# Contrast adjustment on one core: last store in three pieces, first store begun with a piece of its own, bias matmuls in reverse order

## The chip, the cores and the metric

The kernel runs on one core of one Trainium2 chip. The metric is the device time of one execution in microseconds, as the median over several runs. The profile is of one further execution.

## The reference

The input is a batch of 16 images with 3 channels of 512 x 512 float32 pixels, 50.33 MB in all. For each image and channel the mean over its 262,144 pixels is taken, and each pixel is moved away from that mean by a factor of 1.5 and clipped to 0..1.

```python
def reference(x, factor):                       # x: (16, 3, 512, 512) float32, factor 1.5
    mean = np.mean(x, axis=(2, 3), keepdims=True)
    return np.clip(mean + factor * (x - mean), 0, 1).astype(np.float32)
```

## The kernel before

**Tiles.** The pixels are seen as one long row and cut into rows of `ROW` = 16384 floats (64 KB). One row fills one partition, 16 rows make one image channel, and 128 rows make a tile, so a tile is 8.39 MB and holds 8 channels. There are six tiles. Three buffers of a whole tile each (`BUFS` = 3) lie in SBUF, so tile t + 3 uses the buffer of tile t.

**Transfers.** `load` (L75 to L79) is issued by SyncE, named SP in the profile. The first tile is loaded by one DMA; each later one by two, the even rows and the odd rows (`PARTS` = 2), 64 rows of 64 KB each. `store` (L113 to L116) is issued by ScalarE's queue (ACT), also as even rows and odd rows. Loads and stores are thus in two queues, which share the 16 DMA engines; the profile calls them q1 (SP) and q10 (ACT). A tile's buffer is loaded anew as soon as the store of the same rows, three tiles before, has landed; SP waits for that, in its program's order.

**Compute of a tile.** `compute` (L81 to L111) first sums each row: VectorE (DVE) reduces the first 8192 columns (`HALF`) with one instruction into `sums` column 0 (L85), and ScalarE copies the other 8192 in four pieces of 2048 (`JUNK`) into a scratch tile `junk`, each with an accumulated sum into columns 1 to 4 (L91). Then TensorE (PE) multiplies `blockw` with each of the five columns of `sums` and accumulates into `pbias` (L96). `blockw` is a matrix with (1 - factor) / 262144 in blocks of 16 x 16 on its diagonal, so this sums the 16 rows of a channel and gives every row of it the bias (1 - factor) * mean. Each of the five matmuls is two instructions on PE. ScalarE copies the bias out of PSUM (L98).

The last step is factor * x + bias, clipped, in place. VectorE alone does columns 0 to 3839 (`OWN`): multiply and add (L100), then clip (L103). The other columns are in four pieces of 4096, 4096, 2816 and 1536 (`CHUNKS`): ScalarE makes Relu(factor * x + bias) of each (L109), and VectorE takes the minimum with 1 (L110), which is called the clamp below. The store of the tile follows the fourth piece.

**Order.** The instructions of each engine run in the order in which the program records them (`manual_schedule`): three loads, and then for each tile its compute, its store, and the load of the tile after next but one. The waits between engines, for data and for buffers, are put in by the framework. Each DMA counts its completion on one of eight counters, and the next DMA on the same counter waits until the one before it has landed.

Of the kernel before, what the change touches and what calls it, by code (L numbers as in the profile page):

```python
# [1 line left out]

# [4 lines left out]


P = 128  # L10
ROW = 16384
BUFS = 3
HALF = ROW // 2
OWN = 3840
CHUNKS = (4096, 4096, 2816, 1536)
JUNK = 2048
PARTS = 2


@with_exitstack  # L20
def kernel(
    ctx: ExitStack,
    tc: tile.TileContext,
    x: bass.AP,
    factor: float,
    out: bass.AP,
):

    nc = tc.nc
    f32 = mybir.dt.float32
    Alu = mybir.AluOpType
    Act = mybir.ActivationFunctionType

    B, C, H, W = x.shape
    n_img, n_pix = B * C, H * W
    ppi = n_pix // ROW
    per_tile = P // ppi
    n_tiles = n_img // per_tile  # L40
    assert OWN + sum(CHUNKS) == ROW
    assert ppi * ROW == n_pix and per_tile * n_tiles == n_img

    factor = float(factor)
    wconst = (1.0 - factor) / float(n_pix)

    x_f = x.rearrange("b c h w -> (b c h w)")
    out_f = out.rearrange("b c h w -> (b c h w)")

    def dram(ap, t, r, parts):  # L50
        return bass.AP(
            tensor=ap.tensor, offset=(t * P + r) * ROW, ap=[[parts * ROW, P // parts], [1, ROW]]
        )

    consts = ctx.enter_context(tc.tile_pool(name="consts", bufs=1))
    xpool = ctx.enter_context(tc.tile_pool(name="xpool", bufs=1))
    jpool = ctx.enter_context(tc.tile_pool(name="jpool", bufs=1))
    rpool = ctx.enter_context(tc.tile_pool(name="rpool", bufs=2))
    bpool = ctx.enter_context(tc.tile_pool(name="bpool", bufs=2))
    psum = ctx.enter_context(tc.tile_pool(name="psum", bufs=2, space=bass.MemoryType.PSUM))  # L60

    blockw = consts.tile([P, P], f32, name="blockw")
    nc.gpsimd.memset(blockw, 0.0)  # L65
    for a in range(0, P, 2 * ppi):
        mid, end = a + ppi, a + 2 * ppi
        nc.gpsimd.memset(blockw[a:end, mid:end], wconst)  # L68
        nc.gpsimd.memset(blockw[a:mid, mid:end], 0.0)  # L69
        nc.gpsimd.memset(blockw[a:mid, a:mid], wconst)  # L70


    bufs = [xpool.tile([P, ROW], f32, name=f"x{b}") for b in range(BUFS)]

    def load(t):  # L75
        xt = bufs[t % BUFS]
        parts = 1 if t == 0 else PARTS
        for r in range(parts):
            nc.sync.dma_start(out=xt[r::parts, :], in_=dram(x_f, t, r, parts))  # L79

    def compute(t):  # L81
        xt = bufs[t % BUFS]
        n_act = (ROW - HALF) // JUNK
        sums = rpool.tile([P, 1 + n_act], f32, name="sums")
        nc.vector.tensor_reduce(  # L85
            out=sums[:, 0:1], in_=xt[:, 0:HALF], axis=mybir.AxisListType.X, op=Alu.add
        )
        for j in range(n_act):
            junk = jpool.tile([P, JUNK], f32, name="junk")
            a = HALF + j * JUNK  # L90
            nc.scalar.activation(  # L91
                out=junk, in_=xt[:, a : a + JUNK], func=Act.Copy, accum_out=sums[:, 1 + j : 2 + j]
            )
        pbias = psum.tile([P, 1], f32, name="pbias")
        for j in range(1 + n_act):
            nc.tensor.matmul(pbias, blockw, sums[:, j : j + 1], start=j == 0, stop=j == n_act)  # L96
        bias = bpool.tile([P, 1], f32, name="bias")
        nc.scalar.copy(out=bias, in_=pbias)  # L98
        own = xt[:, 0:OWN]
        nc.vector.tensor_scalar(  # L100
            out=own, in0=own, scalar1=factor, scalar2=bias, op0=Alu.mult, op1=Alu.add
        )
        nc.vector.tensor_scalar(  # L103
            out=own, in0=own, scalar1=0.0, scalar2=1.0, op0=Alu.max, op1=Alu.min
        )
        c = OWN
        for n in CHUNKS:
            part = xt[:, c : c + n]
            nc.scalar.activation(out=part, in_=part, func=Act.Relu, bias=bias, scale=factor)  # L109
            nc.vector.tensor_scalar(out=part, in0=part, scalar1=1.0, scalar2=None, op0=Alu.min)  # L110
            c += n  # L111

    def store(t):  # L113
        xt = bufs[t % BUFS]
        for r in range(PARTS):
            nc.scalar.dma_start(out=dram(out_f, t, r, PARTS), in_=xt[r::PARTS, :])  # L116

    with tc.manual_schedule():
        for t in range(min(BUFS, n_tiles)):
            load(t)  # L120
        for t in range(n_tiles):
            compute(t)
            store(t)
            if t + BUFS < n_tiles:
                load(t + BUFS)


# [1 line left out]
_INS = ['x', 'factor']  # L129
_OUTS = [((16, 3, 512, 512), 'float32')]  # L130

_NUMBERS = {'factor': 1.5}


# [26 lines left out]
```

## Time and profile before

| | |
|---|---|
| time, median of 5 runs | 241.49 us (241.22, 241.47, 241.49, 243.47, 247.09) |
| the profiled execution's own time | 240.45 us |
| its span, first to last instruction | 238.4 us |
| granted TensorE clock | 1.00 |
| busy, VectorE / ScalarE / TensorE | 120.3 / 118.1 / 13.7 us |
| moved by the load queue / the store queue | 50.33 / 50.33 MB |
| mean rate over the span | 422 GB/s |
| one reduction of 8192 columns on VectorE (L85) | 8.68 us |
| one sum of 2048 columns on ScalarE (L91), and reading it out | 1.91 us, 0.19 us |
| the five matmuls of a tile (L96) | 2.3 us |
| one Relu of 4096 columns on ScalarE (L109) | 3.70 us |
| one clamp of 4096 columns on VectorE (L110) | 2.29 us |
| one issue of a store on ScalarE's queue (median) | 0.57 us |

The span is shorter than the execution's time by 2.05 us, which lie before the first and after the last instruction. Times in the profile are microseconds from the start of the span. The name of an engine with a q behind it (ACTq, SPq) stands for what its instruction queue does, such as issuing DMAs and waiting for semaphores, and isn't counted as busy time. Landing is the moment at which a DMA's last completion has been counted.

### The profile page before, as it was taken

The numbers are of one execution on the slowest core, as the hardware profiler recorded it, in microseconds if no ns is written. First come the engines' busy times: TensorE is split into PE (matmuls) and PEld (weight loads), VectorE is DVE, ScalarE is ACT, GpSimd is POOL, SyncE is SP. The second block draws the span as 40 slices with busy tenths as digits, with TensorE's granted clock in tenths as the row PEclk, the third lists the DMA queues.
The fourth block names the chain that finished last, engine by engine and source line by source line (L and its number), as shares of the span: only waits on it lengthen the run. The fifth ranks groups of instructions, "written<-read, shape, count | busy, mean of one in ns | idle before, by whom it ended". The sixth has DMA issues, their size and how long they took to land.

```text
span 238.4 us, 354 instructions
## 1 busy us (share of the span) xinstructions
PE 13.7 (6%) x60; PEld 13.3 (6%) x60; DVE 120.3 (50%) x42; ACT 118.1 (50%) x79; POOL 1.4 (1%) x17
## 2 busy tenths in 40 slices
PE   0000030003000030000012000003000001100000
PEld 0000030003000030000012000003000001100000
DVE  0001958995874958400687830195870068783000
ACT  2001949697954959300677910194960066791000
POOL 2000000000000000000000000000000000000000
DMA  9898989899999898989898989999898989898894
GB/s 352 352 528 352 528 352 528 352 352 484 396 451 429 385 495 352 528 352 528 352 518 363 495 385 484 396 429 451 385 495 352 528 352 517 363 517 363 352 528 176
DMA packets 1905, 100.67 MB, mean 422 GB/s; under 512 B 368, under 2 KB 368, under 8 KB 368
## 3 DMA queue, kind: packets, MB, share of 16 engines
q1 hardware_dynamic: 944, 50.33, 49.6%
q10 hardware_dynamic: 960, 50.33, 48.8%
q14 instruction: 1, 0.01, 0.0%
HBM read 50.33 MB, written 50.33 MB: 422 GB/s over the span
## 4 chain that ended last, share of the span: by engine, by line
DMA 34%; DVE 18%; ACT 17%; another core or an unknown queue 10%; issue 7%; PE 4%; DVEq 0%; SPq 0%
DMA out_dram<-x 20%; ACT x L109 16%; DVE sums L85 15%; DMA x<-in_x_dram 14%; PE pbias L96 4%; DVE x L110 4%; DVEq L156 0%; ACT bias L98 0%; SPq L79 0%; DVEq L85 0%
## 5 line engine op out<-in xcount | busy, mean ns | idle before, releaser
L85 DVE TENSOR_REDUCE sums<-x 128x1 f32<-128x8192 f32 x6 | 52.1, 8684 | 74.6 <-DMA x<-in_x_dram 59.7
L91 ACT ACTIVATE junk<-x 128x2048 f32<-128x2048 f32 x24 | 45.8, 1910 | 79.6 <-DMA x<-in_x_dram 76.7
L109 ACT ACTIVATE x<-x,bias 128x4096 f32<-128x4096 f32 (+2 forms) x24 | 67.8, 2898 | 0.2
L110 DVE TENSOR_SCALAR x<-x 128x4096 f32<-128x4096 f32 (+2 forms) x24 | 42.5, 1790 | 5.8 <-ACT x L109 5.8
L96 PE MATMUL pbias<-sums,blockw 128*128 128x1 f32 x60 | 13.7, 354 | 190.1 <-DVE sums L85 190.1
L96 PEld LDWEIGHTS pbias<-sums,blockw 128*128 128x128 f32 x60 | 13.3, 329 | 190.5 <-DVE sums L85 158.9
L100 DVE TENSOR_SCALAR x<-x,bias 128x3840 f32<-128x3840 f32 x6 | 13.3, 2221 | 15.5 <-ACT bias L98 15.5
L103 DVE TENSOR_SCALAR x<-x 128x3840 f32<-128x3840 f32 x6 | 13.0, 2160 | 0.2
L98 ACT COPY bias<-pbias 128x1 f32<-128x1 f32 x6 | 1.0, 160 | 16.6 <-PE pbias L96 16.6
L91 ACT ACTIVATION_READ_ACCUMULATOR junk<-x 128x1 f32 x24 | 4.5, 186 | 0.0
L91 ACT ACT_TABLE_LOAD x1 | 1.3, 1283 | 0.7 <-PEq L142 0.7
L68 POOL MEMSET blockw<- 32x16 f32 x4 | 0.4, 104 | 0.2
L69 POOL MEMSET blockw<- 16x16 f32 x4 | 0.4, 104 | 0.2
L70 POOL MEMSET blockw<- 16x16 f32 x4 | 0.4, 104 | 0.0
L65 POOL MEMSET blockw<- 128x128 f32 x1 | 0.2, 206 | 0.3 <-POOLq L142 0.3
L142 POOL MEMSET const-bfloat16-1.0<- 128x1 bf16 x1 | 0.1, 112 | 0.0
L142 POOL MEMSET const-uint8-127<- 128x1 uint8 x1 | 0.1, 112 | 0.0
L142 POOL MEMSET const-float32-1.0<- 128x1 f32 x1 | 0.1, 108 | 0.0
L142 POOL MEMSET const-float32-0.0<- 128x1 f32 x1 | 0.1, 104 | 0.2 <-issue 0.2
## 6 DMA issues: line engine op xcount, KB each, us to landing
out_dram<-x ACTq DMA_DIRECT2D x12, 40.7
x<-in_x_dram SPq DMA_DIRECT2D x11, 26.1
```

The lines of the kernel that those rows point to most:

```text
L68: nc.gpsimd.memset(blockw[a:end, mid:end], wconst)
L69: nc.gpsimd.memset(blockw[a:mid, mid:end], 0.0)
L70: nc.gpsimd.memset(blockw[a:mid, a:mid], wconst)
L85: nc.vector.tensor_reduce(out=sums[:, 0:1], in_=xt[:, 0:HALF], axis=mybir.AxisListType.X, op=Alu.add)
L91: nc.scalar.activation(out=junk, in_=xt[:, a : a + JUNK], func=Act.Copy, accum_out=sums[:, 1 + j : 2 + j])
L96: nc.tensor.matmul(pbias, blockw, sums[:, j : j + 1], start=j == 0, stop=j == n_act)
L98: nc.scalar.copy(out=bias, in_=pbias)
L100: nc.vector.tensor_scalar(out=own, in0=own, scalar1=factor, scalar2=bias, op0=Alu.mult, op1=Alu.add)
L103: nc.vector.tensor_scalar(out=own, in0=own, scalar1=0.0, scalar2=1.0, op0=Alu.max, op1=Alu.min)
L109: nc.scalar.activation(out=part, in_=part, func=Act.Relu, bias=bias, scale=factor)
L110: nc.vector.tensor_scalar(out=part, in0=part, scalar1=1.0, scalar2=None, op0=Alu.min)
L142: nc = _bacc.Bacc("TRN2", target_bir_lowering=False, num_devices=1)
```

## The change

Three things are changed, and the arithmetic stays the same.

1. The five matmuls of each tile run in reverse order: first ScalarE's fourth sum, then its third, second and first, and VectorE's sum last.
2. The store of the last tile is three DMAs, over all 128 rows, cut by columns: 0 to 7935 (`EARLY` = 7936), behind the third Relu and clamp in the program; then, behind the fourth, 7936 to 12031 (`LATE` = 12032) and 12032 to 16383. Before it was even rows and odd rows, behind the fourth.
3. The store of the first tile begins with columns 0 to 3839 of the even rows (15 KB of each of 64 rows), as a DMA of its own behind the second Relu and clamp. The rest of the even rows and then the odd rows follow behind the fourth.

The stores of the other four tiles are as they were. `store` is now called from within `compute`, with a list of pieces.

```diff
+EARLY = OWN + CHUNKS[0]
+LATE = EARLY + CHUNKS[1]
...
-    def dram(ap, t, r, parts):
+    def dram(ap, t, r, parts, c0=0, c1=ROW):
         return bass.AP(
-            tensor=ap.tensor, offset=(t * P + r) * ROW, ap=[[parts * ROW, P // parts], [1, ROW]]
+            tensor=ap.tensor,
+            offset=(t * P + r) * ROW + c0,
+            ap=[[parts * ROW, P // parts], [1, c1 - c0]],
         )
...
+    def store(t, pieces):
+        xt = bufs[t % BUFS]
+        for r, parts, c0, c1 in pieces:
+            nc.scalar.dma_start(out=dram(out_f, t, r, parts, c0, c1), in_=xt[r::parts, c0:c1])
+    late = len(CHUNKS) - 1
+    def stores(t):
+        if t == n_tiles - 1:
+            return {
+                late - 1: [(0, 1, 0, EARLY)],
+                late: [(0, 1, EARLY, LATE), (0, 1, LATE, ROW)],
+            }
+        if t == 0:
+            rest = [(r, PARTS, 0, ROW) for r in range(1, PARTS)]
+            return {1: [(0, PARTS, 0, OWN)], late: [(0, PARTS, OWN, ROW)] + rest}
+        return {late: [(r, PARTS, 0, ROW) for r in range(PARTS)]}
...
-        for j in range(1 + n_act):
-            nc.tensor.matmul(pbias, blockw, sums[:, j : j + 1], start=j == 0, stop=j == n_act)
+        for j in range(n_act, -1, -1):
+            nc.tensor.matmul(pbias, blockw, sums[:, j : j + 1], start=j == n_act, stop=j == 0)
...
-        for n in CHUNKS:
+        for k, n in enumerate(CHUNKS):
...
             c += n
+            store(t, stores(t).get(k, []))
-    def store(t):
-        xt = bufs[t % BUFS]
-        for r in range(PARTS):
-            nc.scalar.dma_start(out=dram(out_f, t, r, PARTS), in_=xt[r::PARTS, :])
...
             compute(t)
-            store(t)
```

## The prediction

> **What bounds the kernel now.** I began with the page: busy shares, slices, queues.
>
> ```profile
> PE 13.7 (6%) x60; PEld 13.3 (6%) x60; DVE 120.3 (50%) x42; ACT 118.1 (50%) x79; POOL 1.4 (1%) x17
> ...
> DMA  9898989899999898989898989999898989898894
> ```
>
> The first line gives each engine's busy time: none is at work for more than half the span. In the second, a digit is the DMA engines' busy share, in tenths, in a fortieth of the span, 8 or 9 in all but the last. The kernel is bound by its transfers, so the question is where the 16 DMA engines stand still. Busy time by stretch says that.
>
> ```profile
> 46.00:52.00 6.00, 0.00 (x0) 0.00 (x0) 6.00 (x2) 4.17 (x5) 0.00 (x0) 1.00 0.90 295
> 52.00:216.00 164.00, 11.47 (x50) 11.05 (x50) 94.25 (x35) 93.22 (x61) 0.00 (x0) 1.00 1.00 434
> ```
>
> The last three columns are granted clock, DMA share and GB/s. A packet counts where it starts, so short stretches are rough, but from 52 to 216 us the share is 1.00. Nothing that an engine does there can shorten the time. What happens after 216 us I read from the stores' line: first the two stores of tile 4, then the two of tile 5, the last.
>
> ```profile
> L116 ACTq DMA_DIRECT2D out_dram<-x x2: 479/548/617, 177.8 to 178.3; - x2
> ...
> DMA to landing us min/median/max: 30.0/34.6/39.2
> ```
>
> ```profile
> L116 ACTq DMA_DIRECT2D out_dram<-x x2: 479/544/609, 216.4 to 216.9; - x2
> ...
> DMA to landing us min/median/max: 11.4/16.0/20.5
> ```
>
> Issue time plus time to landing gives landings at 207.8 and 217.5 (tile 4), 227.8 and 237.5 (tile 5). Inside a pair the step is 9.7 us, and 4.19 MB in 9.66 us is the 434 GB/s of the full stretch. From tile 4's last landing to tile 5's first it is 10.3. So there is one **bubble** of about 0.64 us (two digits from the trace: 237.47 - 217.51 - 2 x 9.66), because the last store is issued at 216.43, too late to be ready when the queue empties. The timeline shows why.
>
> ```profile
> 200.63 0.19 ACT L91 ACTIVATION_READ_ACCUMULATOR junk<-x 128x1 f32 x1
> 201.50 2.21 PEld L96 LDWEIGHTS pbias<-sums,blockw 128*128 128x128 f32 x10 [36.39 <-DVE sums L85]
> 201.50 2.29 PE L96 MATMUL pbias<-sums,blockw 128*128 128x1 f32 x10 [36.31 <-DVE sums L85]
> 203.83 0.16 ACT L98 COPY bias<-pbias 128x1 f32<-128x1 f32 x1 [3.02 <-PE pbias L96]
> 204.02 2.22 DVE L100 TENSOR_SCALAR x<-x,bias 128x3840 f32<-128x3840 f32 x1 [2.58 <-ACT bias L98]
> 204.02 11.31 ACT L109 ACTIVATE x<-x,bias 128x4096 f32<-128x4096 f32 x4
> 206.28 2.16 DVE L103 TENSOR_SCALAR x<-x 128x3840 f32<-128x3840 f32 x1
> 208.36 2.29 DVE L110 TENSOR_SCALAR x<-x 128x4096 f32<-128x4096 f32 x1
> 211.37 2.29 DVE L110 TENSOR_SCALAR x<-x 128x4096 f32<-128x4096 f32 x1 [0.72 <-ACT x L109]
> 213.90 2.50 DVE L110 TENSOR_SCALAR x<-x 128x2816 f32<-128x2816 f32 x2 [0.24 <-ACT x L109]
> 216.43 1.13 ACTq L116 DMA_DIRECT2D out_dram<-x  x2
> ```
>
> Columns 0 to 7935 are finished at 210.65, and are stored only after the last clamp.
>
> **The change, part by part.** *Reordered matmuls.* ScalarE's four sums are there at 200.63 + 0.19 = 200.82, VectorE's at 201.45. PE now begins with ScalarE's: from about 200.88, four fifths of 2.29 us (1.83) to 202.71, then the fifth (0.46) to 203.17, where it ended at 203.79. That is 0.6 us earlier in every tile but one. In tile 1 ScalarE is the late one (it first issues tile 0's stores; its last sum is there at 55.88), so PE ends at 55.94 + 2.29 = 58.23, not 57.40: 0.8 later, less the 0.6 won in tile 0. By itself the edit is worth nothing before the end, as the DMA engines are full; what covers tile 1's 0.2 is tile 0's second store, which holds the queue until 47.06 + 42.2 = 89.3, against tile 1's issue at 70.03. At the end alone it would take 0.6 out of the bubble.
>
> *Three-piece last store.* Piece one (columns 0 to 7935, 4.06 MB) stands behind the third Relu in ACT's program and waits for the clamp that ended at 210.65; with the 0.6 that is 210.05. Does an issue wait until the Relus before it have run? The stores' line and ACT's timeline around 89 us say no:
>
> ```profile
> L116 ACTq EVENT_SEMAPHORE  x1: 17/17/17, 89.3 to 89.3; - x1
> ```
>
> ```profile
> 86.14 11.31 ACT L109 ACTIVATE x<-x,bias 128x4096 f32<-128x4096 f32 x4
> ```
>
> The first is a wait of tile 2's store, behind all four Relus in the program, and it passes at 89.3 while those run, from 86.14 to 97.45. Bounds for the issue are therefore 210.05 and the end of the third Relu, 213.9 - 0.6 = 213.3. A lone store takes 11.4 us for 9.66 us of bytes, 1.7 us on top, so piece one is ready by 211.8 or 215.0, both ahead of 217.5, and the bubble is gone by either. I take 210.05, which leaves 5.7 us of cover. Behind the issue, on ACT, stands the fourth Relu (needed at about 213.3) and, behind that, pieces two and three: an issue takes 0.48 to 0.61 us, so it holds nothing. Piece two is ready by 213.66 - 0.6 + 1.7 = 214.8, piece three by 216.4 - 0.6 + 0.6 + 1.7 = 218.1, while piece one alone runs from 217.5 to 226.9. Piece two also waits for the last user of its completion counter, tile 2's second store, landed since 166.7. Saved: 0.64 us.
>
> *More, shorter rows.* Each DMA engine now gets 24 rows of 16 to 32 KB for the last store in place of 8 of 64 KB, and one DMA more; the first store has 4 rows and one DMA more. The trace has no such rows. From below: back-to-back stores land 9.66 us apart, which is their bytes and nothing more, so the price of a seam is 0. From above: each of the two added DMAs pays a lone store's 1.7 us, 3.4 in all. These pieces stand in a queue behind others, as the 9.66 us stores do, and not alone: I take 0.
>
> A rule of the Trainium skill speaks against this part (page "DMA: Bandwidth & Descriptors", section "Anatomy of one DMA"): a DMA costs a fixed 2.0 us or so besides its bytes. Read as a charge on each DMA, it would make two more of them 4.0 us and the sum 3.4 us worse than before; the 9.66 us step between this kernel's queued stores shows no such charge.
>
> *Early piece of the first store.* Its 15 KB of the 64 even rows (0.98 MB, 2.27 us at 434 GB/s) are finished when the second own operation ends, 38.50 - 0.6 = 37.9, and by the same run-ahead are issued there, at the latest behind the second Relu (about 40.8). Until now the store went out at 46.48. The bytes are the same, so with full engines the total doesn't move; loads move back by up to 2.27 us. Late next would be tile 1's second load: landed at 1.73 + 40.3 = 42.0, now by 44.3, needed when tile 0 is done, 46.37 - 0.6 = 45.8: covered. SP's reload of the even rows waits for both pieces. Were the whole 2.27 us handed on to tile 5's load (192.7), piece one would still be ready 3.4 us before the queue empties.
>
> One thing here has a price that I can't see. From 42.1 (tile 1's landing) to 217.5 the engines move 75.5 MB, 173.9 us of work in 175.4, and the one stretch below full share is 46 to 52 us, when the store queue is first used: 1.5 us are lost there, once. With a short first piece that loss may vanish (-1.5) or be paid at both issues (+1.5). I take it as paid once as before: 0.
>
> **Sum.** 240.45 (the profiled execution: its span of 238.4 and 2.05 around it) - 0.64 = 239.8, with a span of 237.7. The median of the runs, 241.49, is 1.04 above the profiled one; on its scale the forecast is 240.9.
>
> **Rivals.**
> - *Seams (slower).* Between pieces of the last store, and at the first store's, the engines idle. For it: nothing in this trace has rows this short. Against it: the 9.66 us step. Price 2 x 1.7 - 0.64 = +2.8, 244.3; it decides from 0.32 us a seam.
> - *The first-use loss is paid twice.* +1.5 - 0.64: 242.4. For it: two issues 8 us apart, the first with little in it. Against: four more stores are issued after 52 us, and the share stays at 1.00.
> - *The first-use loss vanishes* behind the short piece: -1.5 - 0.64: 239.4. For it: what it hits is the load packet ahead of the first store packet. Against: no row shows a cheaper start.
> - *The change doesn't do what it says:* loads come later, piece one comes late, the bubble stays: 241.5. It needs 5.7 us of delay where the edit moves 2.27.
>
> **How the numbers follow.** Forecast 0.60, seams 0.10, loss twice 0.12, loss gone 0.12, bubble stays 0.06. The range reaches down to the vanished loss and up over the doubled one and the nearer half of the seams: 239.3 to 243.3. One per cent, 2.4 us, is about what a measurement of this kernel can tell from no change; the bubble and the whole first-use loss together come to 2.1, so faster by over 1% has only the edge of the vanished loss, 0.05, slower (most of the seams) 0.09, within 1% 0.86.
>
> **What would show it.** Right: tile 5's first piece issued near 210 and landing some 9.4 us after tile 4's last store, the last landing near 236.8, PE's block beginning at ScalarE's sums, the early piece issued near 38. Wrong: a DMA share under 1.00 between 217 and 236, or a longer dip around 40 to 52. The forecast fails if pieces land further apart than their bytes at 434 GB/s.

## The result, and the profile after

The changed kernel's median is 240.68 us over 44 runs (239.43 to 244.95), beside 242.84 us over 79 runs of the kernel before (240.38 to 247.61). Executions over 1.5% longer than the fastest of the same kernel, here 21 of the 79 and 5 of the 44, are left out of this and all later ratios. The ratio is 0.994, with a 95% interval of 0.9925 to 0.9956: some 1.1 to 1.8 us faster, about 1.45. That is inside one per cent and inside the range, but 1.7 to 2.8 times the 0.64 us of the forecast. The median of the five runs shown for the kernel before, 241.49, was low beside that of the 79, so it is luck that the forecast's 240.9 is near to the measured time: the forecast change was too small.

The profiled execution that came with the result took 243.42 us, longer than most; the profile shown here is of another execution of the same kernel (240.51 us, span 238.4), from the last set of experiments. First its page: busy time, slices, packets.

```profile
PE 13.7 (6%) x60; PEld 13.2 (6%) x60; DVE 120.3 (50%) x42; ACT 118.1 (50%) x79; POOL 1.4 (1%) x17
...
DMA  9898989879998989898998989898989898998994
...
DMA packets 2257, 100.67 MB, mean 422 GB/s; under 512 B 400, under 2 KB 400, under 8 KB 400
```

The engines do the same work as before and the DMA engines are as full. The 2257 packets are 352 more than the 1905 of before: 22 more on each of the 16 DMA engines, which are the shorter rows and two more completions. The busy time by stretch (length, engines, granted clock, DMA share, GB/s) has moved in the first of the two stretches:

```profile
46.00:52.00 6.00, 0.00 (x0) 0.00 (x0) 6.00 (x1) 4.85 (x5) 0.00 (x0) 1.00 1.02 431
52.00:216.00 164.00, 11.47 (x50) 11.04 (x50) 93.81 (x35) 92.54 (x61) 0.00 (x0) 1.00 1.00 432
```

The dip of 46 to 52 us (before: share 0.90, 295 GB/s) is gone from that place; packets are counted where they start, so its size has to come from the packets themselves, below. Then the stores, first the two of tile 4, and after them the three pieces of tile 5: issue times, and time from issue to landing.

```profile
L88 ACTq DMA_DIRECT2D out_dram<-x x2: 479/650/822, 177.1 to 177.7; - x2
...
DMA to landing us min/median/max: 31.3/35.9/40.4
```

```profile
L88 ACTq DMA_DIRECT2D out_dram<-x x3: 338/338/354, 210.5 to 216.2; - x3
...
DMA to landing us min/median/max: 17.0/18.8/21.3
```

Tile 4 ends at 177.7 + 40.4 = 218.1. The pieces are issued at 210.5, 213.5 and 216.2 and land at 227.5, 232.3 and 237.5. The steps are 9.4, 4.8 and 5.2 us, and their bytes at 434 GB/s are 9.4, 4.8 and 5.1: no pause is left ahead of the last store or within it. The timeline of the last tile shows how the first piece comes to be ready:

```profile
201.07 0.19 ACT L115 ACTIVATION_READ_ACCUMULATOR junk<-x 128x1 f32 x1
201.31 2.21 PEld L121 LDWEIGHTS pbias<-sums,blockw 128*128 128x128 f32 x10 [36.88 <-ACT junk L115]
201.31 2.29 PE L121 MATMUL pbias<-sums,blockw 128*128 128x1 f32 x10 [36.79 <-ACT junk L115]
203.64 0.16 ACT L123 COPY bias<-pbias 128x1 f32<-128x1 f32 x1 [2.38 <-PE pbias L121]
203.83 7.31 ACT L134 ACTIVATE x<-x,bias 128x4096 f32<-128x4096 f32 x2
...
208.16 2.29 DVE L135 TENSOR_SCALAR x<-x 128x4096 f32<-128x4096 f32 x1
210.48 0.35 ACTq L88 DMA_DIRECT2D out_dram<-x  x1
211.04 2.63 ACT L134 ACTIVATE x<-x,bias 128x2816 f32<-128x2816 f32 x1
```

PE's wait now ends on ScalarE's sum (201.07 + 0.19) where it ended on VectorE's. The issue at 210.48 follows the clamp that ended at 210.45, while the second Relu still runs (until 203.83 + 7.31 = 211.14) and before the third one, which stands ahead of it in the program, has begun: issues run ahead of the queued Relus. The same is seen for tile 0's early piece:

```profile
33.44 7.31 ACT L134 ACTIVATE x<-x,bias 128x4096 f32<-128x4096 f32 x2
...
37.89 0.56 ACTq L88 DMA_DIRECT2D out_dram<-x  x1
40.66 4.09 ACT L134 ACTIVATE x<-x,bias 128x2816 f32<-128x2816 f32 x2
```

### The profile page after: what moved, and what is told of

Same layout as the page of the kernel before. It is cut to its first block, busy times and chain, and to the rows that moved or that the text cites. A ratio compares the mean times of both kernels' runs of the same rounds, so it can differ in the third digit from the quotient of the medians.

```text
span 241.4 us, 359 instructions
## 1 busy us (share of the span) xinstructions
PE 13.7 (6%) x60; PEld 13.2 (5%) x60; DVE 120.2 (50%) x42; ACT 118.2 (49%) x79; POOL 1.4 (1%) x17
## 2 busy tenths in 40 slices
DMA packets 2257, 100.67 MB, mean 417 GB/s; under 512 B 400, under 2 KB 400, under 8 KB 400
## 4 chain that ended last, share of the span: by engine, by line
DMA 37%; another core or an unknown queue 24%; ACT 21%; PE 3%; DVE 3%; issue 1%; SPq 1%; ACTq 0%; DVEq 0%
DMA x<-in_x_dram 21%; DMA out_dram<-x 15%; ACT x L134 11%; ACT junk L115 10%; PE pbias L121 3%; DVE x L135 3%; SPq L83 1%; ACTq L88 0%; DVEq L176 0%; ACT bias L123 0%; ACTq L115 0%
```

## The experiments

Ratios are against the kernel before in the same set, with their 95% interval. There were three sets of four kernels, each on one chip; the first ran on another chip than the second, and that on another than the third. The whole change was not among the first set's kernels, so those parts are compared with it only across chips.

### First set: each part by itself

The matmul order alone:

```diff
-        for j in range(1 + n_act):
-            nc.tensor.matmul(pbias, blockw, sums[:, j : j + 1], start=j == 0, stop=j == n_act)
+        for j in range(n_act, -1, -1):
+            nc.tensor.matmul(pbias, blockw, sums[:, j : j + 1], start=j == n_act, stop=j == 0)
```

> The kernel before with the matmuls in reverse order and nothing else. Theory A (the gain is the fixed bubble of 0.64 us before the last store, plus some 0.5 us that the first store's early piece saves where the store queue is first used): the last store is issued 0.6 us earlier, near 215.8, the bubble shrinks from 0.64 to about 0.0 us and the time falls by 0.6 us; a dip of the first store stays at 1.2 to 1.5 us. Theory B (in most executions of the kernel before, the bubble is larger than in its profiled one, because the last load lands later beside the store queue): also 0.6 us faster, but a bubble of 1 us or more is left in the trace.

Measured: 0.9994 (0.9964 to 1.0023). In the traced execution PE began with ScalarE's sum and the last store was issued at 215.85. Tile 4's last store landed at 177.1 + 42.0 = 219.1 and tile 5's first at 215.8 + 13.0 = 228.8, one store of 9.7 us later. So no pause was left, and none of the 1 us that theory B wanted. The time shows no gain; the 0.6 us of both theories (0.9975) lie inside the interval and can't be excluded by it.

The three-piece last store alone (`stores` without its branch for tile 0, matmuls in the old order):

```diff
-        if t == 0:
-            rest = [(r, PARTS, 0, ROW) for r in range(1, PARTS)]
-            return {1: [(0, PARTS, 0, OWN)], late: [(0, PARTS, OWN, ROW)] + rest}
```

> The three-piece last store alone, with the matmuls in the old order and the first store as before. Theory A: 0.6 us faster, no bubble, the same 1.2 to 1.5 us lost at the first store. Theory B: the whole gain of the change or more, 1.4 to 2 us, since this part alone covers a bubble of any size up to some 5 us.

Measured: 0.9996 (0.9956 to 1.0035). Theory B, by which this part alone brings 1.4 to 2 us (0.994 to 0.992), falls. Theory A's 0.6 us isn't excluded, but no gain is seen.

The early piece alone (`stores` without its branch for the last tile, matmuls in the old order):

```diff
-        if t == n_tiles - 1:
-            return {
-                late - 1: [(0, 1, 0, EARLY)],
-                late: [(0, 1, EARLY, LATE), (0, 1, LATE, ROW)],
-            }
```

> The early piece of the first store alone. Theory A: 0.5 us faster, with the load packets under way at the first issue taking about 2.7 us in place of 3.7, and the bubble before the last store still there. Theory B: no change in time (within 0.3 us), or the bubble larger or smaller by a packet of 2.4 us, as the order of loads and stores moves.

Measured: 0.9991 (0.9958 to 1.0025). The packets moved as theory A said: the 16 load packets just ahead of the first store packets took 2.75 us on average, where the first profile of the kernel before has 3.71 for them and 2.42 for the others around. But the last store waits longer than before: tile 4 ends at 178.3 + 39.7 = 218.0 and the next landing is at 217.7 + 11.4 = 229.1, 11.1 us later where the bytes take 9.7. The pause is 1.4 us, where the first profile of the kernel before has 0.64; by this one trace, what was saved at the start is given back at the end.

The whole without its early piece (the `t == 0` branch left out, the rest as after):

> The change without the early piece of the first store: three-piece last store and matmuls in reverse order. Theory A: 0.6 us faster than before, as the three-piece store alone (the two take out the same bubble), and 0.5 us slower than the whole change. Theory B: as fast as the whole change, within 0.3 us.

Measured: 0.9987 (0.9948 to 1.0027). Neither a part nor this pair showed a gain, while the whole had 0.994. That gave a new theory, C: the two stores' edits need each other.

### Second set: the pairs with the early piece

The whole change once more:

> The whole change once more, for a second execution's trace beside the kernels of this call. Theory C (the early piece saves some 0.5 us where the store queue is first used, but moves the last load about 2 us later beside the stores, so that a bubble of 1.2 us opens before an unsplit last store; the three-piece last store covers that; the two parts need each other): 1.0 to 1.5 us faster than before, no bubble, first-use loss of 0.7 us per DMA engine, and the last store starting 24 us after the last load's landing without a pause. Theory D (the gain is scatter between executions and chips, and no part does anything): within 0.5 us of before.

Measured: 0.9938 (0.9895 to 0.998), as in the first comparison, on another chip than the parts above. Theory D, scatter alone, is out: the interval leaves out 1 on this chip too. The traced execution has 0.8 us of loss at first use and no pause.

Early piece and three-piece last store, with the matmuls in the old order:

> The change without the reversed matmuls: early piece and three-piece last store. Theory C: as the whole change within 0.3 us, since the three-piece store has 5 us of cover and needs nothing from the 0.6 us of the matmuls. Rival E (the matmul order is what makes the whole work): 0.6 us or more slower than the whole change.

Measured: 0.992 (0.9883 to 0.9957): as the whole. Its last store is issued at 210.65 in the trace, when the queue still has over 7 us of tile 4 to send (until 218.0). The matmul order isn't needed for the gain, and rival E falls.

Early piece and matmul order, with the last store as even and odd rows:

> The change without the three-piece last store: early piece and reversed matmuls. Theory C: first-use loss of 0.7 us as in the whole, but a bubble of about 0.6 us left before the last store (1.2 less the 0.6 of the matmuls), so some 0.6 us slower than the whole change. Theory D or E: as the whole change.

Measured: 0.9927 (0.9891 to 0.9963). The trace shows the pause that C expects, 0.8 us (tile 4 ends at 218.9, the next landing is at 229.3), but the time isn't 0.6 us worse than the whole. The interval, 0.4% to either side, is too wide to say that this contradicts the pause; it doesn't support C. All three kernels of this set with the early piece are equally fast, which would also fit a gain by the early piece alone; that kernel didn't run on this chip.

The kernel before once more:

> The kernel before once more, for a second trace. Theory C: 1.2 to 1.3 us lost per DMA engine at the first store; the last load's landing lies 24.8 to 26.6 us ahead of the end of tile 4's stores, and so a bubble of 0 to 0.7 us, differing from execution to execution. Theory B (bubble of most executions is larger than in the first profile): over 1 us.

Measured: 0.9986 (0.9931 to 1.0042) against itself, which is how far two sets of the same kernel lie apart. Its traced execution is the fastest of its twelve, 239.61 us. The two stores of tile 4 and the two of tile 5, from its stores' line:

```profile
L116 ACTq DMA_DIRECT2D out_dram<-x x2: 479/547/615, 175.8 to 176.3; - x2
...
DMA to landing us min/median/max: 31.9/36.5/41.1
```

```profile
L116 ACTq DMA_DIRECT2D out_dram<-x x2: 479/548/617, 214.4 to 214.9; - x2
...
DMA to landing us min/median/max: 12.7/17.2/21.8
```

Tile 4 ends at 176.3 + 41.1 = 217.4 and tile 5's first half lands at 214.4 + 12.7 = 227.1, 9.7 us later. **This execution of the unchanged kernel has no pause at all.** The 0.64 us that the forecast wanted to remove belong to the first profiled execution, not to the kernel.

### Third set: the halves again, on one chip with the whole

The early piece alone:

> The early piece of the first store alone, on the chip of the whole change. Theory C (the two stores' edits need each other): first-use loss near 0.7 us, a pause of about 1 us ahead of the last store, and at most 0.5 us faster than before, at least 0.7 us slower than the whole change of this call. Theory F (the early piece alone makes the gain, by keeping the DMA engines in step; the earlier figures differ only by the chip they ran on): as fast as the whole change within 0.4 us.

Measured: 0.9986 (0.9951 to 1.0022). Its stores of tile 4 and tile 5:

```profile
L88 ACTq DMA_DIRECT2D out_dram<-x x2: 478/544/610, 177.8 to 178.4; - x2
...
DMA to landing us min/median/max: 30.3/34.9/39.4
```

```profile
L88 ACTq DMA_DIRECT2D out_dram<-x x2: 479/544/609, 217.2 to 217.7; - x2
...
DMA to landing us min/median/max: 11.4/15.9/20.5
```

From 217.8 to 228.6 are 10.8 us for 9.7 of bytes: a pause of 1.1 us, as C expects, and 11.4 us from issue to landing, the time of a store that finds the queue empty. Theory F, by which the early piece alone makes the gain, isn't borne out: two sets have the early piece alone at 0.9991 and 0.9986, three have the whole at 0.993 to 0.994, though the intervals of this set overlap (the means of the runs compared are 241.20 us for the early piece alone and 240.76 for the whole). So F isn't excluded.

The change without the early piece:

> The change without the early piece, on the chip of the whole change. Theory C: first-use loss of 1.2 us, no pause ahead of the last store, 0.5 us or more slower than the whole change. Theory F: no faster than before (within 0.4 us), 1.2 us or more slower than the whole change.

Measured: 1.0022 (0.9989 to 1.0054), against 0.9934 for the whole in the same set; the two intervals don't touch. The pieces come early enough,

```profile
L88 ACTq DMA_DIRECT2D out_dram<-x x3: 338/338/357, 211.0 to 216.8; - x3
...
DMA to landing us min/median/max: 18.6/20.4/22.9
```

and land at 229.6, 234.4 and 239.7, without a pause, but 2.1 us later than the whole's, because tile 4 already ended at 177.9 + 42.4 = 220.3. The time is lost earlier: the first DMA engine to complete tile 4's last store does so 0.5 us later than in the whole's trace (216.5 against 216.0), and the last one follows it by 3.7 us in place of 2.0.

The whole change, as the measure of this set:

> The whole change once more, as the measure of its parts in this call: 1.2 to 1.8 us faster than before by either theory.

Measured: 0.9934 (0.9897 to 0.9972). This is the execution shown at the head.

The whole with a smaller early piece:

```diff
-            return {1: [(0, PARTS, 0, OWN)], late: [(0, PARTS, OWN, ROW)] + rest}
+            return {1: [(0, PARTS, 0, 960)], late: [(0, PARTS, 960, ROW)] + rest}
```

> The whole change, but the early piece of the first store is 960 columns (3.75 KB of each of 64 rows) in place of 3840. If the loss at the first use of the store queue goes with the size of the first store rows (1.25 us with 64 KB, 0.3 us at the first 15 KB row), the load packet under way at the first issue takes at most 2.5 us, and the loss comes at the later, large piece: in all 0.7 to 1.3 us. If it is a fixed cost of first use, some 0.7 us in all as with 15 KB. The time: as the whole change within 0.5 us by either.

Measured: 0.9944 (0.9907 to 0.9981), as the whole. The load packets just ahead of the small piece's rows took 2.42 us, as any other; those ahead of the large piece's took 3.39. In all the first use cost 1.0 us per DMA engine. So the loss isn't a fixed price of first use: it came with the large rows. Here the early piece saved at most 0.3 us of it, and the time shows no smaller gain for that; the interval, 0.4% to either side, is too wide to say more. Neither this kernel nor the pair of early piece and three-piece store is measurably better than the whole, so no version that beats it was found.

### The packets and the spread, side by side

From the packets' and completions' records in the traces, one execution each. "First use" is the time that load packets took beyond 2.42 us between 30 and 72 us, per DMA engine. "Pause" is the landing of tile 5's first part, less that of tile 4's last, less its bytes. "Spread" is the time between the first and the last DMA engine to complete tile 4's last store. The last row is the execution that came with the result.

| kernel | first use, us | pause, us | spread, us |
|---|---|---|---|
| before, first profile | 1.3 | 0.6 | 0.9 |
| before, second profile | 1.2 | 0 | 0.9 |
| matmul order alone | 1.3 | 0 | 2.6 |
| three-piece last store alone | 1.1 | 0 | 3.1 |
| both of these, two executions | 1.2, 1.1 | 0, 0 | 4.0, 3.7 |
| early piece alone, two executions | 0.7, 0.8 | 1.4, 1.1 | 2.0, 1.6 |
| early piece and matmul order | 0.9 | 0.8 | 2.4 |
| early piece and three-piece store | 0.8 | 0 | 1.9 |
| the whole, two executions | 0.8, 0.6 | 0, 0 | 1.7, 2.0 |
| the whole, small early piece | 1.0 | 0 | 0.8 |
| the whole, at 243.42 us | 0.7 | 0 | 5.0 |

The spread weighs most. In all fourteen traces the first DMA engine to complete tile 4's last store does so between 216.0 and 216.6 us, and the last landing of all comes after the spread, the pause and 19.3 to 19.4 us for tile 5's bytes. So the spans, 237.5 to 241.4 us, differ mainly by the spread, and by up to 1.4 us of pause. The two traces of the kernel before, with spans of 238.4 and 237.6, are no longer than those of the whole, 238.3, 238.4 and 241.4: they caught short executions (240.45 and 239.61 us, beside a median of 242.84), and none shows what a usual one loses.

## Why the prediction was right, and where not

**Right.** Transfers bound the kernel, and finishing the sums earlier gained nothing that could be measured: the matmul order alone has 0.9994. PE begins with ScalarE's sums; issues run ahead of the Relus (37.89 and 210.48); the last store is ready with several us to spare; the last landing came at 237.5, where 236.8 was forecast for an execution like the first profiled one. The price of more, shorter rows, put at 0, is nearly that: a 16 KB row took 0.611 us where a quarter of a 64 KB row is 0.605, so each row costs some 6 ns, and the 16 further rows on each engine 0.13 us in all. The rival of the seams is excluded by the steps of 9.4, 4.8 and 5.2 us. So is the reading of the Trainium skill's rule (page "DMA: Bandwidth & Descriptors", section "Anatomy of one DMA", which gives it for DMAs issued by GpSimd, where these are issued by ScalarE) as a charge of 2.0 us on each DMA: between queued pieces no such charge shows; a store that finds the queue empty, at 11.4 us for 9.7 us of bytes, pays 1.7 us.

**Wrong step one: "Saved: 0.64 us".** The bubble was read off one execution, as if it were the kernel's. In the second trace it is 0, and the three-piece store alone shows no gain (0.9996). Where one to three of the 16 DMA engines lag by 2 to 4 us, as in the traces of the parts without the early piece, a late last store is late for the other engines only; those that lag still have tile 4's rows to send and don't wait, and they set the end. What the piece does save appears with the early piece beside it: there the unsplit last store pauses for 0.8 to 1.4 us, and the split one doesn't. In times, the early piece alone has 0.9991 and 0.9986, and together with the three-piece store 0.992 to 0.994, for the most part on different chips.

**Wrong step two: "I take it as paid once as before: 0".** The loss at the first use of the store queue fell from 1.1 to 1.3 us to 0.6 to 0.9, so some 0.5 us were gained here, a third of the way to the rival in which it vanishes. The small early piece shows that the loss is neither fixed nor gone: it came with the 60 KB rows, and 1.0 us of it stayed.

**Half right: "loads move back by up to 2.27 us".** They do, by up to one packet in the turn of the two queues. On the first DMA engine to complete, tile 5's load ends 24.2 to 25.0 us ahead of tile 4's last store in the traces with the 15 KB early piece (191.5 and 216.0 us in the one shown), and 25.8 to 26.6 us ahead in those without it (190.0 and 216.5 in the second trace of the kernel before); with the small one it is 26.5 us. I counted this against the cover of the split store, where it does no harm, and missed that with an unsplit last store it opens a pause, as in the three such traces. That would explain why the early piece alone shows no gain and the pair does, but the times don't bear it out: the early piece with reversed matmuls has the pause, too, and was as fast as the whole, within 0.4%.

**What stays open.** First use (about 0.5 us) and the pause that the split store covers (about 1 us, of which the kernel before has 0 to 0.6) explain at most 1.1 of the 1.45 us. Nor do they explain that two kernels were as fast as the whole: the early piece with the reversed matmuls, which has the pause, and the small early piece, which keeps most of the loss at first use and doesn't move the load. So the cause of the gain isn't shown. The spread between DMA engines looks smaller with the early piece (0.8 to 2.4 us) than in the parts without it (2.6 to 4.0), and it counts fully at the end where there is no pause; but the two traces of the kernel before have 0.9, one of the whole has 5.0, and one execution of each can't settle a quantity that differs from execution to execution. That the early piece keeps the engines in step is therefore a guess, and so is that a usual execution of the kernel before is longer by its spread; traces of usual executions, and all parts on one chip, would be needed. Nor was the share of the matmul order measured closer than to 0.3%.

## What to carry to other kernels

A pause found in one profile belongs to that execution until a second one shows it; profile the unchanged kernel twice before pricing it. Two edits on a full transfer queue may show nothing each and a gain together (0.999, 0.9996 and 0.992 here, though partly on different chips), and the one can open a pause that the other covers, so try them as a pair before dropping either, on the same chip as the parts. And where rows are dealt out to DMA engines in equal shares, the engine that lags sets the end: average shares and mean rates don't show it, the first and last completion of one transfer do.

## What the runs showed of the hardware that I had not expected

When store packets first join a DMA engine that is sending loads, the load packet just ahead of them is stretched: on average over the 16 engines from 2.42 to between 3.5 and 3.7 us with 64 KB store rows, to between 2.5 and 3.2 with 15 KB rows, and not measurably with 3.75 KB. It can be paid again when a larger row follows (2.4 to 3.1 us ahead of the 49 KB rows, 3.39 ahead of the 60 KB ones).

Single packets, nearly all of them loads, are stretched in the same way later, up to 3.3 us. After 72 us these stretches, the time beyond 2.42 us, come to 1.0 to 1.4 us, summed over all engines, in the three traces with a spread under 1 us, and to 2.6 to 10.3 us in the others. That fits a spread made of them; the traces here don't name the engine of a packet, so it isn't shown. In the 243.42 us execution of the whole change, one DMA engine completed tile 4's last store 5.0 us after the first one had, where the execution shown has 2.0, and the last landing came 3.0 us later (240.5 against 237.5).
